# A macaron block with hybrid sparse attention on one Trainium2 core: attention's TensorE order held as written, position adds on GpSimd, compression jobs and first loads rearranged

## The chip, the cores and the metric

The kernel runs on one core of one Trainium2 chip. The metric is device time in microseconds of a run. Three runs of the kernel before took 1013.84 (median), 1013.3 and 1014.18. One execution was profiled; it is the source of all rows below.

## The reference

One transformer layer on 512 tokens of width 1024, float32. Everything is computed at float32 accuracy.

```python
x = x + 0.5 * swiglu(rmsnorm(x, norm_ffn1), w_gate1, w_up1, w_down1)      # 1024 -> 2816 -> 1024
x = x + hybrid_mixer(rmsnorm(x, norm_mix), w_in, ..., w_out, rel_bias)
x = x + 0.5 * swiglu(rmsnorm(x, norm_ffn2), w_gate2, w_up2, w_down2)
return rmsnorm(x, norm_final)

# hybrid_mixer: h @ w_in gives q, k, v of 8 MoBA heads (width 64), q of 8 NSA heads,
# two groups each of raw, selected and window k and v, and 24 gates
def compress(raw, pos, w1, w2):                # blocks of 32 tokens, every 16: 31 blocks
    blocks = raw[:, :, idx] + pos
    return silu(blocks.reshape(B, G, n_cmp, 32 * dh) @ w1) @ w2
# NSA: gates[0] * softmax over the 31 compressed blocks
#    + gates[1] * softmax over selected blocks of ks, vs + gates[2] * softmax over a window of kw, vw
# MoBA: softmax over the selected blocks and the own block; both with a relative position bias
# o = concat(heads) @ w_out
```

With 512 tokens every block is selected, so both the selected and the window branch are causal attention over all tokens.

## The kernel before, in words

**Products.** A float32 product is made of three matmuls (`mm3`, L86 to L89: L87, L88 and L89 are its three) on a high and a low part of each factor. A weight chunk is loaded by SyncE into one of three `raw` buffers; `halves` splits it: `whi` by ScalarE (ACT, L81), `wlo` by VectorE (DVE, L82), or by GpSimd (POOL) once `side[0]` is set, which is so during attention. Activations `x` are kept as eight tiles of 128 features by 512 tokens, and as pairs `xo` (high, low).

**The FFNs.** `Ffn.go` (L380 to L413) writes a list of steps out in order, with loads, sums and splits started ahead by fixed costs, and holds TensorE to that order: `tc.manual_schedule(engines={PE})`. `begun` (L416) makes the first steps, the six plain blocks, and hangs "posts" on them: work for other engines that is issued behind a given step. `sums_of_x` (L187) and `blocks_of_x` make what the later, mixed blocks need; `squares_of_tokens`, `roots` and `rows_of_roots` make 1/rms: a reciprocal on DVE (L150) and eight transpositions of it on TensorE into `pR` (L156). FFN1's first loads are written out by hand on SyncE's queue: `first_x` and `first_w`, then the four token tiles, then the third weight and x4 to x7.

**The mixer's projections.** All products of the normalized x with `w_in`, the compression and the output product are "jobs": a load and a generator that yields after each `mm3`. `stream` runs the jobs of the lists `pre`, `fill` and `last`, loading two ahead. `proj(i, then)` gives one 128-feature projection `pp`; `token_major` gives values `vn` and `vm` (tiles `pv`, copied with a factor by ACT L683 and DVE L684). `compress` gives for k and v each a projection whose `blocks` add the positions (L711, eight adds on DVE into a `raw` buffer), four hidden jobs (`pc`, ending in a silu into `hid`, L735 to L737), and `second`: two transpositions into `pct` (L745), splits, and a small product `pck`. `moved` (L607) copies halves of partitions by SyncE's queue: eight moves for a k (`stack_k`), four for a q pair (`stack_q`). The list `pre` is run to its end, `need("vc")`, before attention begins; in it the hidden jobs alternate with projections.

**Attention.** 72 steps of `chunks_of_head`: three for each of 24 passes (NSA heads 8 to 15 with ks and kw, MoBA heads 0 to 7), and four more of `cmp_pair` for the compressed branch. Each has a logits part (TensorE L900, L901 into `ps_s`; DVE L908 adds the bias `tb` and reduces to a maximum; ACT L910 exponential; DVE L915 reciprocal; POOL L921 gating), a turn (transpositions into `ps_t`, L930, copied to `th` by ACT L933 and `tl` by DVE L934), and values (L93, L94 into `po`). The loop issues the logits of step i, the turn of step i-4 and the values of step i-7, and after each a number of `mm3` of the job list, by the table `share`. So the job list fills TensorE between attention's parts. `ahead` and `need` force jobs that a head wants. In the kernel before, the program's scheduler, not this loop alone, sets the order of all engines here.

Of the kernel before, what the change touches and what calls it, by code (L numbers as in the profile page):

```python
# [18 lines left out]
NK = D // 128  # L19
# [13 lines left out]
def block_kernel(ctx: ExitStack, tc: tile.TileContext, A: dict, out: bass.AP):  # L33
# [382 lines left out]
    def begun(ffn, w, posts):  # L416

        steps = [s for f in range(0, PLAIN, 3) for s in ffn.plain(range(f, f + 3))]
        sums = [(at, lambda k=k: ffn.sums_of_x(k)) for k, at in enumerate((4, 6, 8, 10))]
        blocks = [(at, lambda k=k: ffn.blocks_of_x(k)) for k, at in enumerate((4, 18, 18, 23))]  # L420
        for at, post in posts + sums + blocks:
            steps[at].post.append(post)
        fills = ffn.down(w, range(PLAIN), half_added, "mm", 2)
        return steps + fills[:LEAD], fills[LEAD:]
# [46 lines left out]
    with ExitStack() as ph:  # L471
# [31 lines left out]
        first_w(1, [slice(0, 8)], nc.sync)  # L503
        tokens = [ffn.raw().rearrange("p a b c -> p (a b c)") for _ in range(NT)]
        for i in range(NT):
            nc.sync.dma_start(tokens[i], A["x"][i * 128:(i + 1) * 128])
        first_w(2, [slice(0, 8)], nc.sync)
        for k in range(4, NK):
            first_x(k)
# [23 lines left out]
        def then(d, p):  # L533
# [4 lines left out]
        steps, fills = begun(ffn, A["wd1"], [  # L538
            (1, squares_of_tokens), (2, lambda: roots(0, ss[:, 0])), (3, lambda: rows_of_roots(0, "mm")),
# [18 lines left out]
    with ExitStack() as ph:  # L558
# [140 lines left out]
        def compress(which):  # L699
# [3 lines left out]
            def blocks(p):  # L703
                tv = scaled(p, None).rearrange("p (n s) -> p s n", s=16)
                xt = chunk((16, 64))
                xv = xt.rearrange("p l (g n) -> p l g n", g=2)
                nc.gpsimd.memset(xv[:, :, :, 31:32], 0.0)
                for g in range(2):
                    for l in range(2):
                        for e in range(2):  # L710
                            nc.vector.tensor_tensor(  # L711
                                xv[half(l), 8 * e:8 * e + 8, g, 0:31], tv[half(g), l:16:2, e:e + 31],
                                pos[half(g), which, 16 * e + l:16 * e + 16:2].unsqueeze(2).to_broadcast([64, 8, 31]),
                                ALU.add)
                for l0 in range(0, 16, 4):
                    t = akt().rearrange("p (l e n) -> p l e n", l=4, e=2)
                    nc.scalar.activation(t[:, :, 0], xt[:, l0:l0 + 4], AF.Copy)
                    nc.vector.tensor_tensor(t[:, :, 1], xt[:, l0:l0 + 4], f32(t[:, :, 0]), ALU.subtract)
                    xc.extend(t[:, l].rearrange("p e n -> p (e n)") for l in range(4))
# [235 lines left out]
        def cmp_pair(pair):  # L955
# [38 lines left out]
            def values():  # L994
# [14 lines left out]
        pre = [kproj, *vn, khid[0], proj(10, nsa_k("ks")), khid[1], vm[0], khid[2], vproj, khid[3], vm[1], ksec,  # L1009
               vhid[0], vm[2], vhid[1], proj(11, nsa_k("kw")), vhid[2], proj(12, nsa_q(0)), vhid[3], vm[3], vsec]  # L1010
        fill = [proj(12 + i, nsa_q(i)) for i in range(1, 4)]
        for i in range(4):
            fill += [proj(2 * i, moba_t("q", i)), proj(2 * i + 1, moba_t("k", i))]
            if i == 2:
                fill += [w_out(d, 4, 8) for d in range(NK)]
# [29 lines left out]
        need("vc")  # L1045
# [29 lines left out]
        for i in range(len(steps) + 7):  # L1075
            for j, lag in enumerate((0, 4, 7)):
                if 0 <= i - lag < len(steps):
                    steps[i - lag][j]()
                run(max(0, int(target[i] + share[i] * (j + 1) / 3) - done[0]))
            if i in starts:  # L1080
                ahead(starts[i])
        for _ in work:
            pass
# [4 lines left out]
    with ExitStack() as ph:  # L1088
# [7 lines left out]
        steps, fills = begun(ffn, A["wd2a"], [  # L1096
            (2, lambda: roots(2, sums_of_squares("mm"))), (3, lambda: rows_of_roots(2, "mm"))])
# [156 lines left out]
```

## Time and profile before

| what | value |
|---|---|
| runs | 1013.3, 1013.84, 1014.18 us |
| profiled execution: time | 1012.73 us |
| profiled execution: span of its instructions | 1010.9 us |
| mean granted TensorE clock | 0.995 |
| TensorE matmuls | 5944 |
| first matmul of attention's stage, first of FFN2 | 434.04 us, 653.35 us |

All stamps are microseconds from the first instruction of the span. The order of stages is FFN1 to about 355, projections and compression to 434, attention to 653, FFN2 and the last norm to the end. A row of a timeline reads: start, duration, engine, line of the code, operation, what it writes and reads, shapes; in brackets the idle time just before it and what ended it. A window row reads: its bounds, its length, the busy time of PE (matmuls), PEld (weight loads), DVE, ACT and POOL with their counts, the granted TensorE clock, the DMA engines' busy share and GB/s.

### The profile page before, as it was taken

Reading aid. Unit: us, or ns where it says so; the run is one execution under the profiler, and the core shown is the slowest. Engines: PE = TensorE matmul, PEld = TensorE weight load, DVE = VectorE, ACT = ScalarE, POOL = GpSimd, SP = SyncE. Lnnn points to the kernel's source line nnn. Section 1 sums busy time; section 2 is a strip of 40 time slices with the busy share of each in tenths; the row PEclk is TensorE's granted clock in tenths of the full one; section 3 lists DMA queues with packets and bytes.
Section 4 is the critical chain, followed back from the end, with each engine's and each line's share of the span. In section 5 each row is a group of like instructions: output and inputs, shape, how many; then the busy total and the mean of one; then the engine's idle time right before and its main releaser. Section 6 shows DMA issues by size and latency. Waiting matters only on the chain.

```text
span 1010.9 us, 15557 instructions
## 1 busy us (share of the span) xinstructions
PE 983.3 (97%) x5944; PEld 862.5 (85%) x5944; DVE 718.7 (71%) x1135; ACT 504.8 (50%) x869; POOL 131.9 (13%) x167
## 2 busy tenths in 40 slices
PE   9999999999999999999999999889999999999997
PEld 7789989999999888788778787778899999999995
DVE  5986676777775675578787866777957777767743
ACT  7554343444433453467676856635534443444444
POOL 0000000000000220035554462600000000000002
PEclk9999999999999999999999999999999999999999
DMA  8533266333211135652132433353243323332102
GB/s 313 219 120 99 90 188 186 110 99 109 88 60 42 45 93 170 192 178 74 48 95 70 123 102 84 120 213 105 84 126 104 105 88 103 124 122 87 43 1 84
DMA packets 45742, 113.86 MB, mean 113 GB/s; under 512 B 10049, under 2 KB 14866, under 8 KB 45668
## 3 DMA queue, kind: packets, MB, share of 16 engines
q1 hardware_dynamic: 45380, 112.73, 36.0%
q8 instruction: 47, 0.77, 0.3%
q14 instruction: 27, 0.22, 0.1%
q10 hardware_dynamic: 288, 0.14, 0.1%
HBM read 100.08 MB, written 5.30 MB: 104 GB/s over the span
## 4 chain that ended last, share of the span: by engine, by line
PE 82%; DVE 6%; DMA 4%; ACT 2%; issue 2%; POOL 1%; SPq 1%; DVEq 0%; ACTq 0%; POOLq 0%
PE pd L87 8%; PE pd L88 8%; PE pd L89 8%; PE pu L89 6%; PE pu L87 6%; PE pu L88 6%; PE pw L87 4%; PE pw L88 4%; PE pw L89 4%; PE pgu L89 3%; PE pgu L87 3%; PE pgu L88 3%; PE pp L87 2%; PE pp L88 2%; PE pp L89 2%
## 5 line engine op out<-in xcount | busy, mean ns | idle before, releaser
L197 ACT ACTIVATE sph<-aw 128x1024 fp32r<-128x1024 f32 x114 | 120.9, 1061 | 237.0 <-PE pu L88 118.6
L81 ACT ACTIVATE whi<-raw 128x1024 fp32r<-128x1024 f32 (+3 forms) x115 | 111.9, 975 | 124.5 <-PE pd L88 30.7
L198 DVE TENSOR_TENSOR spl<-aw,sph 128x1024 fp32r<-128x1024 f32 x114 | 139.3, 1222 | 36.6 <-ACT sph L197 36.5
L82 DVE TENSOR_TENSOR wlo<-raw,whi 128x1024 fp32r<-128x1024 f32 (+3 forms) x91 | 110.9, 1222 | 28.8 <-ACT whi L81 28.0
L88 PE MATMUL pd<-h,whi 128*128 128x512 f32 x320 | 126.4, 395 | 0.0
L87 PE MATMUL pd<-h,whi 128*128 128x512 f32 x320 | 126.2, 394 | 0.0
L89 PE MATMUL pd<-h,wlo 128*128 128x512 f32 x320 | 125.2, 391 | 0.0
L89 PE MATMUL pu<-th,spl 128*128 128x256 f32 x384 | 106.9, 278 | 0.0
L87 PE MATMUL pu<-th,sph 128*128 128x256 f32 x384 | 106.9, 278 | 0.0
L88 PE MATMUL pu<-tl,sph 128*128 128x256 f32 x384 | 106.8, 278 | 0.0
L287 DVE TENSOR_TENSOR aw<-aw 128x1024 f32<-128x1024 f32 x64 | 78.1, 1220 | 33.1 <-DMA aw<-in_wgu 33.1
L469 DVE SCALAR_TENSOR_TENSOR x<-pd,x 128x512 f32<-128x512 f32 x72 | 49.4, 689 | 45.8 <-PE pd L89 45.6
L89 PE MATMUL pgu<-xo,wlo 128*128 128x512 f32 x192 | 74.9, 390 | 1.6 <-DVE wlo L82 1.6
L88 PEld LDWEIGHTS pu<-tl,sph 128*128 128x128 f32 x384 | 72.6, 189 | 4.0
L87 PEld LDWEIGHTS pu<-th,sph 128*128 128x128 f32 x384 | 72.1, 188 | 4.3
L87 PE MATMUL pgu<-xo,whi 128*128 128x512 f32 x192 | 75.3, 392 | 0.4 <-ACT xo L123 0.4
L88 PE MATMUL pgu<-xo,whi 128*128 128x512 f32 x192 | 75.0, 390 | 0.6 <-DVE xo L124 0.6
L89 PEld LDWEIGHTS pu<-th,spl 128*128 128x128 f32 x384 | 72.1, 188 | 0.0
L89 PEld LDWEIGHTS pd<-h,wlo 128*128 128x128 f32 x320 | 60.2, 188 | 13.4
L89 PE MATMUL pw<-xo,spl 128*128 128x256 f32 x256 | 70.9, 277 | 0.0
L87 PE MATMUL pw<-xo,sph 128*128 128x256 f32 x256 | 70.8, 277 | 0.0
L88 PE MATMUL pw<-xo,sph 128*128 128x256 f32 x256 | 70.8, 277 | 0.0
(254 smaller groups left out, 2432.7 us busy)
## 6 DMA issues: line engine op xcount, KB each, us to landing
aw<-in_wgu SPq DMA_DIRECT2D x64, 512.0 KB, 3.9
raw<-in_wgu SPq DMA_DIRECT2D x23, 512.0 KB, 4.6
raw<-in_wd SPq DMA_DIRECT2D x22, 512.0 KB, 3.7
raw<-in_wd2a SPq DMA_DIRECT2D x18, 512.0 KB, 3.7
raw<-in_w_a SPq DMA_DIRECT2D x16, 512.0 KB, 3.6
raw<-in_w SPq DMA_DIRECT2D x8, 512.0 KB, 3.7
aq<-xo SPq DMA_DIRECT2D x32, 128.0 KB, 2.3
raw<-in_w_o SPq DMA_DIRECT2D x16, 256.0 KB, 2.6
```

Of the source, the lines that this page charges most:

```text
L81: nc.scalar.activation(hi[:, s], src[:, s], AF.Copy)
L82: (nc.gpsimd if side[0] else nc.vector).tensor_tensor(lo[:, s], src[:, s], f32(hi[:, s]), ALU.subtract)
L87: nc.tensor.matmul(p, w[0], v[0], start=first, stop=False, skip_group_check=again)
L88: nc.tensor.matmul(p, w[0], v[1], start=False, stop=False, skip_group_check=again)
L89: nc.tensor.matmul(p, w[1], v[0], start=False, stop=last, skip_group_check=again)
L197: nc.scalar.activation(hi, v, AF.Copy)
L198: nc.vector.tensor_tensor(lo, v, f32(hi), ALU.subtract)
L287: nc.vector.tensor_tensor(to, x, y, op)
L469: nc.vector.scalar_tensor_tensor(xs[d], p, 0.5, xs[d], ALU.mult, ALU.add)
```

## The change

- **TensorE's order in attention.** The loop stands in `tc.manual_schedule(engines={PE})`; other engines are still scheduled. The table `share` gives MoBA steps 0.6 for 0.85, drops 2.0 after each MoBA start, adds 3.0 after heads 1, 3 and 5 begin, and 1.2 to the last steps.
- **Jobs.** The hidden jobs of k start later, so that two other jobs stand ahead; the last two of v stand side by side at the end; `vsec`, the second part of v's compression, goes from the end of `pre` into `fill`. A job `marked` ends `pre`. Half of the output jobs of pair 2 go behind pair 3. The splits and moves of the NSA q pairs 2 and 3 are put off to heads 11 and 13.
- **Position adds.** The eight adds of a `blocks` go from DVE to GpSimd, and from a `raw` buffer to the `spare` tiles that `halves_of_rows` uses.
- **FFN starts.** 1/rms is posted two steps later in FFN1 and its rows one step later in FFN2; sums of x begin at step 6 and 5 for 4. FFN1's third weight, x4 to x7 and the second half of block 0 are loaded ahead of the tokens.

```diff
-    def begun(ffn, w, posts):
+    def begun(ffn, w, first, posts):
-        sums = [(at, lambda k=k: ffn.sums_of_x(k)) for k, at in enumerate((4, 6, 8, 10))]
-        blocks = [(at, lambda k=k: ffn.blocks_of_x(k)) for k, at in enumerate((4, 18, 18, 23))]
+        sums = [(first + 2 * k, lambda k=k: ffn.sums_of_x(k)) for k in range(4)]
+        blocks = [(at, lambda k=k: ffn.blocks_of_x(k)) for k, at in enumerate((first, 18, 18, 23))]
...
         first_w(1, [slice(0, 8)], nc.sync)
+        first_w(2, [slice(0, 8)], nc.sync)
+        for k in range(4, NK):
+            first_x(k)
+        ffn.early[0, 1] = chunk((8, 128))
+        nc.sync.dma_start(ffn.early[0, 1], A["wgu1"][0][:, 1].rearrange("p a b c -> p (a b) c"))
         tokens = [ffn.raw().rearrange("p a b c -> p (a b c)") for _ in range(NT)]
...
-        first_w(2, [slice(0, 8)], nc.sync)
-        for k in range(4, NK):
-            first_x(k)
...
-            (1, squares_of_tokens), (2, lambda: roots(0, ss[:, 0])), (3, lambda: rows_of_roots(0, "mm")),
+            (3, squares_of_tokens), (4, lambda: roots(0, ss[:, 0])), (5, lambda: rows_of_roots(0, "mm")),
...
             def then(p):
                 t = scaled(p, 0.125)
-                got["n", pair] = stack_q(t)
+                got["t", pair] = t
+                if pair < 2:
+                    nsa_split(pair)
             return then
+        def nsa_split(pair):
+            got["n", pair] = stack_q(got["t", pair])
...
-                xt = chunk((16, 64))
-                xv = xt.rearrange("p l (g n) -> p l g n", g=2)
-                            nc.vector.tensor_tensor(
-                                xv[half(l), 8 * e:8 * e + 8, g, 0:31], tv[half(g), l:16:2, e:e + 31],
+                xt = [f32(v).rearrange("p (l n) -> p l n", l=8) for v in spare[which]]
+                            nc.gpsimd.tensor_tensor(
+                                xv[half(l), :, g, 0:31], tv[half(g), l:16:2, e:e + 31],
...
-        pre = [kproj, *vn, khid[0], proj(10, nsa_k("ks")), khid[1], vm[0], khid[2], vproj, khid[3], vm[1], ksec,
-               vhid[0], vm[2], vhid[1], proj(11, nsa_k("kw")), vhid[2], proj(12, nsa_q(0)), vhid[3], vm[3], vsec]
-        fill = [proj(12 + i, nsa_q(i)) for i in range(1, 4)]
+        pre = [kproj, *vn, proj(10, nsa_k("ks")), vm[0], khid[0], vproj, khid[1], vm[1], khid[2],
+               proj(11, nsa_k("kw")), khid[3], vm[2], ksec, vhid[0], proj(12, nsa_q(0)), vhid[1], vm[3], vhid[2], vhid[3],
+               (None, marked)]
+        fill = [proj(13, nsa_q(1)), vsec, proj(14, nsa_q(2)), proj(15, nsa_q(3))]
...
-            if i == 2:
-                fill += [w_out(d, 4, 8) for d in range(NK)]
+            if i >= 2:
+                fill += [w_out(d, 4, 8) for d in range(4 * i - 8, 4 * i - 4)]
...
+            if h in (11, 13):
+                need(("t", (h - 7) // 2))
+                nsa_split((h - 7) // 2)
...
-        need("vc")
+        need("pre")
...
-        share = [0.65 if i < n_nsa else 0.85 for i in range(len(steps) + 7)]
+        share = [0.65 if i < n_nsa else 0.6 for i in range(len(steps) + 7)]
-                if i >= n_nsa:
-                    share[i + 1] += 2.0
+            if starts.get(i) in (1, 3, 5):
+                share[i + 1] += 3.0
+        for i in range(len(steps) - 3, len(steps) + 7):
+            share[i] += 1.2
...
+        with tc.manual_schedule(engines={mybir.EngineType.PE}):
+            for i in range(len(steps) + 7):
...
-            (2, lambda: roots(2, sums_of_squares("mm"))), (3, lambda: rows_of_roots(2, "mm"))])
+            (2, lambda: roots(2, sums_of_squares("mm"))), (4, lambda: rows_of_roots(2, "mm"))])
```

Where the instructions stand now, at three places.

TensorE, the first steps of attention. `ps_s` are logits, `pp` a projection's matmuls that fill, `ps_t` the first turn. The turn's last transposition reads `lp_4256`, the softmax of the third logits. Before, 29 other rows follow those logits, and then come:

```order
L87 MATMUL pp_4435<-xo_3456,whi_4181 128x512
L900 MATMUL ps_s_4299<-kvn_4056,aq_4117 128x512
L901 MATMUL ps_s_4299<-kvn_4058,aq_4117 128x512
L88 MATMUL pp_4435<-xo_3457,whi_4181 128x512
L89 MATMUL pp_4435<-xo_3456,wlo_4182 128x512
L87 MATMUL pp_4435<-xo_3467,whi_4181 128x512
L88 MATMUL pp_4435<-xo_3468,whi_4181 128x512
L89 MATMUL pp_4435<-xo_3467,wlo_4182 128x512
L87 MATMUL pp_4604<-xo_3352,whi_4220 128x512
L88 MATMUL pp_4604<-xo_3353,whi_4220 128x512
L930 MATMUL ps_t_4287<-ident_84,lp_4256 128x128
```

In the changed kernel, from the third logits (`ps_s_4215`, whose softmax is `lp_4216`) on:

```order
L908 MATMUL ps_s_4215<-kvn_3746,aq_4089 128x512
L909 MATMUL ps_s_4215<-kvn_3748,aq_4089 128x512
L908 MATMUL ps_s_4223<-kvn_3955,aq_4089 128x128
L909 MATMUL ps_s_4223<-kvn_3957,aq_4089 128x128
L908 MATMUL ps_s_4223<-kvn_3955,aq_4089 128x256
L909 MATMUL ps_s_4223<-kvn_3957,aq_4089 128x256
L87 MATMUL pp_4211<-xo_3361,whi_4163 128x512
L88 MATMUL pp_4211<-xo_3362,whi_4163 128x512
L89 MATMUL pp_4211<-xo_3361,wlo_4164 128x512
L908 MATMUL ps_s_4237<-kvn_3955,aq_4089 128x384
L909 MATMUL ps_s_4237<-kvn_3957,aq_4089 128x384
L938 MATMUL ps_t_4247<-ident_84,lpn_4182 128x128 x2
```

The turn comes nine rows after the third logits, and its four transpositions stand together: two more rows of it, the second reading `lp_4216`, follow.

ACT at the same place. `vm` are the copies of the last value chunk, `whi` splits of weights, `hid` the hidden layer of v's compression, L918 (L910 before) the exponentials. Before:

```order
L735 ACTIVATE hid_4133<-pc_3970 64x256
L737 ACTIVATE hid_4133<-hid_4133 64x256
L81 ACTIVATE whi_4181<-raw_4179 128x1024
L683 ACTIVATE vm_4167<-pv_3795,rc1_94 128x8x64
L683 ACTIVATE vm_4168<-pv_3796,rc1_94 128x8x64
L683 ACTIVATE vm_4169<-pv_3797,rc1_94 128x8x64
L683 ACTIVATE vm_4170<-pv_3798,rc1_94 128x8x64
L81 ACTIVATE whi_4220<-raw_4218 128x1024
L750 ACTIVATE hh_4188<-pct_4185 128x128
L756 ACTIVATE w2h_4194<-w2_4192 128x128
L910 ACT_TABLE_LOAD
L910 ACTIVATE lpn_4229,m_4234<-lpn_4229,m_4234 128x128
```

In the changed kernel, from the last copy on:

```order
L690 ACTIVATE vm_4144<-pv_3769,rc1_94 128x8x64
L81 ACTIVATE whi_4163<-raw_4161 128x1024
L81 ACTIVATE whi_4207<-raw_4205 128x1024
L743 ACTIVATE hid_4175<-pc_4047 64x256
L81 ACTIVATE whi_4398<-raw_4396 128x1024
L918 ACT_TABLE_LOAD
L918 ACTIVATE lpn_4182,m_4187<-lpn_4182,m_4187 128x128
L918 ACTIVATE lpn_4182,m_4187<-lpn_4182,m_4187 128x256
L918 ACTIVATE lpn_4196,m_4187<-lpn_4196,m_4187 128x384
L745 ACT_TABLE_LOAD
L745 ACTIVATE hid_4175<-hid_4175 64x256
L918 ACT_TABLE_LOAD
```

The silu of `hid` stood ahead of the copies and of all exponentials; it stands now between the third and the fourth exponential of the first pass, with a table load on either side.

DVE at the start of FFN1. L187 are the sums of x, L82 splits of weights, L124 the low parts of x. Before:

```order
L124 SCALAR_TENSOR_TENSOR xo_196<-x6_76,gcol_69,xo_195 128x512
L187 SCALAR_TENSOR_TENSOR xa_310<-x0_70,gcol_69,R_100 128x512
L187 SCALAR_TENSOR_TENSOR xb_311<-x4_74,gcol_69,R_100 128x512
L187 SCALAR_TENSOR_TENSOR xa_363<-x1_71,gcol_69,R_100 128x512
L187 SCALAR_TENSOR_TENSOR xb_364<-x5_75,gcol_69,R_100 128x512
L187 SCALAR_TENSOR_TENSOR xa_405<-x2_72,gcol_69,R_100 128x512
L187 SCALAR_TENSOR_TENSOR xb_406<-x6_76,gcol_69,R_100 128x512
L124 SCALAR_TENSOR_TENSOR xo_200<-x7_77,gcol_69,xo_199 128x512
L448 TENSOR_TENSOR tabl_92<-tabs_89,tabh_91 33x16
L188 TENSOR_TENSOR xa_310<-xa_310 128x256
L82 TENSOR_TENSOR wlo_275<-raw_205,whi_274 128x1024
```

In the changed kernel:

```order
L124 SCALAR_TENSOR_TENSOR xo_198<-x6_76,gcol_69,xo_197 128x512
L124 SCALAR_TENSOR_TENSOR xo_202<-x7_77,gcol_69,xo_201 128x512
L82 TENSOR_TENSOR wlo_269<-raw_150,whi_268 128x1024
L446 TENSOR_TENSOR tabs_89<-tabs_89,far_90 32x16
L448 TENSOR_TENSOR tabl_92<-tabs_89,tabh_91 33x16
L150 RECIPROCAL rc0_93<-rc0_93 128x4
L82 TENSOR_TENSOR wlo_307<-raw_207,whi_306 128x1024
L82 TENSOR_TENSOR wlo_366<-raw_234,whi_365 128x1024
L187 SCALAR_TENSOR_TENSOR xa_341<-x0_70,gcol_69,R_100 128x512
L187 SCALAR_TENSOR_TENSOR xb_342<-x4_74,gcol_69,R_100 128x512
```

The six sums stood ahead of a split; three splits stand ahead of the sums now.

More of the change, by code (lines that the diff above doesn't have):

```diff
@@ L536, in then @@
             squares(tmp, d, "tmp", 3)
-        steps, fills = begun(ffn, A["wd1"], [
-            (1, squares_of_tokens), (2, lambda: roots(0, ss[:, 0])), (3, lambda: rows_of_roots(0, "mm")),
+        steps, fills = begun(ffn, A["wd1"], 6, [
+            (3, squares_of_tokens), (4, lambda: roots(0, ss[:, 0])), (5, lambda: rows_of_roots(0, "mm")),
             (12, make_rows)])
@@ L704, in blocks @@
                 tv = scaled(p, None).rearrange("p (n s) -> p s n", s=16)
-                xt = chunk((16, 64))
-                xv = xt.rearrange("p l (g n) -> p l g n", g=2)
[L707 to L711, printed above, removed]
-                                xv[half(l), 8 * e:8 * e + 8, g, 0:31], tv[half(g), l:16:2, e:e + 31],
+                xt = [f32(v).rearrange("p (l n) -> p l n", l=8) for v in spare[which]]
+                for e in range(2):
+                    xv = xt[e].rearrange("p l (g n) -> p l g n", g=2)
+                    nc.gpsimd.memset(xv[:, :, :, 31:32], 0.0)
+                    for g in range(2):
+                        for l in range(2):
+                            nc.gpsimd.tensor_tensor(
+                                xv[half(l), :, g, 0:31], tv[half(g), l:16:2, e:e + 31],
                                 pos[half(g), which, 16 * e + l:16 * e + 16:2].unsqueeze(2).to_broadcast([64, 8, 31]),
@@ L715, in blocks @@
                 for l0 in range(0, 16, 4):
+                    v = xt[l0 // 8][:, l0 % 8:l0 % 8 + 4]
                     t = akt().rearrange("p (l e n) -> p l e n", l=4, e=2)
-                    nc.scalar.activation(t[:, :, 0], xt[:, l0:l0 + 4], AF.Copy)
-                    nc.vector.tensor_tensor(t[:, :, 1], xt[:, l0:l0 + 4], f32(t[:, :, 0]), ALU.subtract)
+                    nc.scalar.activation(t[:, :, 0], v, AF.Copy)
+                    nc.vector.tensor_tensor(t[:, :, 1], v, f32(t[:, :, 0]), ALU.subtract)
                     xc.extend(t[:, l].rearrange("p e n -> p (e n)") for l in range(4))
@@ L1008, in block_kernel, with marked @@
         vm = token_major("vm", A["w_v"], 512, vm_tiles)
-        pre = [kproj, *vn, khid[0], proj(10, nsa_k("ks")), khid[1], vm[0], khid[2], vproj, khid[3], vm[1], ksec,
-               vhid[0], vm[2], vhid[1], proj(11, nsa_k("kw")), vhid[2], proj(12, nsa_q(0)), vhid[3], vm[3], vsec]
-        fill = [proj(12 + i, nsa_q(i)) for i in range(1, 4)]
+        def marked(w):
+            got["pre"] = True
+            yield
+        pre = [kproj, *vn, proj(10, nsa_k("ks")), vm[0], khid[0], vproj, khid[1], vm[1], khid[2],
+               proj(11, nsa_k("kw")), khid[3], vm[2], ksec, vhid[0], proj(12, nsa_q(0)), vhid[1], vm[3], vhid[2], vhid[3],
+               (None, marked)]
+        fill = [proj(13, nsa_q(1)), vsec, proj(14, nsa_q(2)), proj(15, nsa_q(3))]
         for i in range(4):
             fill += [proj(2 * i, moba_t("q", i)), proj(2 * i + 1, moba_t("k", i))]
-            if i == 2:
-                fill += [w_out(d, 4, 8) for d in range(NK)]
+            if i >= 2:
+                fill += [w_out(d, 4, 8) for d in range(4 * i - 8, 4 * i - 4)]
         both = []
@@ L1070, in block_kernel @@
                 share[i + 7] += 2.0
-                if i >= n_nsa:
-                    share[i + 1] += 2.0
+            if starts.get(i) in (1, 3, 5):
+                share[i + 1] += 3.0
+        for i in range(len(steps) - 3, len(steps) + 7):
+            share[i] += 1.2
         target = [sum(share[:i]) for i in range(len(share) + 1)]
[L1075 to L1083, printed above, removed]
+        with tc.manual_schedule(engines={mybir.EngineType.PE}):
+            for i in range(len(steps) + 7):
+                for j, lag in enumerate((0, 4, 7)):
+                    if 0 <= i - lag < len(steps):
+                        steps[i - lag][j]()
+                    run(max(0, int(target[i] + share[i] * (j + 1) / 3) - done[0]))
+                if i in starts:
+                    ahead(starts[i])
+            for _ in work:
+                pass
         xg = [got["x", d] for d in range(NK)]
@@ L1094, in block_kernel @@
         hs = ffn.hs
-        steps, fills = begun(ffn, A["wd2a"], [
-            (2, lambda: roots(2, sums_of_squares("mm"))), (3, lambda: rows_of_roots(2, "mm"))])
+        steps, fills = begun(ffn, A["wd2a"], 5, [
+            (2, lambda: roots(2, sums_of_squares("mm"))), (4, lambda: rows_of_roots(2, "mm"))])
         for f in range(PLAIN, NF, FP):
```

## The prediction

> **What bounds the kernel now.** I read the page's shares first, then windows by stage, then TensorE's waits, then timelines at the gaps.
>
> ```profile
> span 1010.9 us, 15557 instructions
> PE 983.3 (97%) x5944; PEld 862.5 (85%) x5944; DVE 718.7 (71%) x1135; ACT 504.8 (50%) x869; POOL 131.9 (13%) x167
> ```
>
> TensorE (PE) is busy 97% of the span, and the change leaves its 5944 matmuls alone. What can go is its idle time, 27.6 us, and time at a lowered clock. The windows by stage (columns: length, then busy time of PE, weight loads, DVE, ACT, POOL, then granted clock) say where that lies:
>
> ```profile
> 50.00:350.00 300.00, 300.00 (x1978) 272.67 (x1977) 211.48 (x246) 128.75 (x174) 4.90 (x6) 1.00 0.34 105
> 355.00:434.00 79.00, 74.55 (x396) 63.55 (x395) 49.02 (x67) 37.13 (x58) 6.44 (x5) 0.96 0.54 163
> 434.00:653.40 219.40, 209.97 (x1152) 172.83 (x1152) 168.62 (x441) 147.52 (x361) 110.38 (x139) 1.00 0.35 93
> 675.00:975.00 300.00, 300.00 (x1975) 273.23 (x1974) 217.75 (x266) 130.64 (x176) 0.00 (x0) 1.00 0.30 94
> 373.00:383.00 10.00, 7.64 (x29) 5.89 (x28) 7.46 (x15) 5.52 (x14) 0.00 (x0) 0.83 0.41 125
> 403.00:413.00 10.00, 7.91 (x28) 5.70 (x27) 6.12 (x11) 5.54 (x10) 0.00 (x0) 0.83 0.60 178
> ```
>
> The two FFNs lose nothing in their 300 us stretches. The projections before attention (355 to 434) lose 4.45 us at two places, both followed by a granted clock of 0.83. Attention (434 to 653.4) shows 9.4 us idle. The list of PE's waits (line, releaser, total, times, longest) gives the names:
>
> ```profile
> PE pR L156 <- DVE rc L150: 2.9, 1, 2.9
> PE ps_s L900 <- DVE m L908: 2.9, 9, 0.6
> PE pp L89 <- DVE wlo L82: 2.4, 1, 2.4
> PE pct L745 <- ACT hid L737: 1.8, 1, 1.8
> PE pgu L89 <- DVE wlo L82: 1.6, 1, 1.6
> ```
>
> Four single waits carry 8.7 us; attention's are many and short. The list understates a wait, because a matmul's shown duration overlaps the next one:
>
> ```profile
> 434.04 0.39 PE L87 MATMUL pp<-xo,whi 128*128 128x512 f32 x1
> 470.00 0.40 PE L88 MATMUL pp<-xo,whi 128*128 128x512 f32 x1
> 470.23 0.39 PE L89 MATMUL pp<-xo,wlo 128*128 128x512 f32 x1
> 653.35 0.39 PE L87 MATMUL pgu<-xo,whi 128*128 128x512 f32 x1
> ```
>
> Undisturbed 512-column matmuls start 0.23 us apart (470.00 and 470.23) and show 0.40. I therefore count losses from start to start. From the first of attention's 1152 matmuls (434.04) to the first after them (653.35), the excess of each spacing over that of its shape, taken where it passes 0.08 us, adds to 23 us: 9.4 visible, the rest inside shown durations. About 8 of it lies in 610 to 640, the rest mostly in 500 to 570.
>
> **FFN1's start.** Matmul 25.50 is followed by one at 27.44: 1.94 us where 0.23 is due, 1.7 lost.
>
> ```profile
> 25.50 0.39 PE L88 MATMUL pgu<-xo,whi 128*128 128x512 f32 x1
> 27.44 0.50 PE L89 MATMUL pgu<-xo,wlo 128*128 128x512 f32 x1 [1.56 <-DVE wlo L82]
> 26.18 1.21 DVE L82 TENSOR_TENSOR wlo<-raw,whi 128x1024 fp32r<-128x1024 f32 x1
> ```
>
> The DVE split at 26.18 stands behind six sums (L187, about 0.7 us each). In the changed order three weight splits stand ahead of those sums. The x and third-weight loads also move ahead of the tokens; the squares that need tokens are posted two steps later. I take the whole 1.7. Bounds: 0, if the token loads, now later, hold the rows of 1/rms; 3, if the earlier half of block 0 also removes small waits.
>
> **Projections: two stalls go, a small one comes.**
>
> ```profile
> 370.88 4.34 DVE L711 TENSOR_TENSOR raw<-t,pos 64x248 f32<-64x248 f32 x8
> L139 POOL TENSOR_TENSOR acc<-acc,sq 128x512 f32<-128x512 f32 x14 | 22.4, 1598 | 16.1 <-ACT sq L138 15.9
> 641.58 1.56 DVE L124 SCALAR_TENSOR_TENSOR xo<-x,gcol,xo 128x512 fp32r<-128x512 f32 x1 [0.80 <-ACT xo L123]
> 637.73 0.76 DVE L124 SCALAR_TENSOR_TENSOR xo<-x,gcol,xo 128x512 fp32r<-128x512 f32 x1 [0.33 <-ACT xo L123]
> ```
>
> The eight position adds hold DVE for 4.34 us, and the split that PE wants stands behind them. Idle 2.36 plus 0.17 x 10 of lost clock makes 4.1 us in the window 373 to 383. On GpSimd an add of 248 columns is not in the trace; by L139 (1.6 us for 512) it costs about 0.8, so eight cost 6.4, against a first consumer (the first hidden job) that now stands one projection plus one chunk of the value projection later, about 10 us of PE work. Without that cover the adds would cost 6.4 at each of two calls. The second stall (403 to 413: idle 2.09 plus 1.7 of clock, 3.8) is the silu of the hidden layer, read at once, together with weight loads queued behind eight moves. In the new job order the moves stand behind three loads, and the first silu has a value chunk and its own projection between. I take both away, 7.9, and add 0.45 at the last value chunk, where two hidden jobs now stand side by side: 7.4 saved (bounds 3 and 8).
>
> A DVE op took 0.76 alone and 1.56 beside a GpSimd op (641.58). By the Trainium skill, "SBUF — State Buffer", section "SBUF: two separate sides", a DVE op with two SBUF inputs and a GpSimd op that reads SBUF lock each other out wholly; the two durations agree. By rows, DVE would stand still for up to 2 x 6.4 = 12.8 us; it is busy 49 of 79 us here, so I put that at nothing as long as the 10 us cover holds.
>
> **FFN2's start.**
>
> ```profile
> 664.96 0.39 PE L89 MATMUL pgu<-xo,wlo 128*128 128x512 f32 x1
> 668.29 0.38 PE L156 MATMUL pR<-ident,rc 128*128 128x128 f32 x1 [2.95 <-DVE rc L150]
> 666.92 1.23 DVE L287 TENSOR_TENSOR aw<-aw 128x1024 f32<-128x1024 f32 x1 [5.79 <-DMA aw<-in_wgu]
> ```
>
> 3.33 us pass where 0.23 is due. The reciprocal waits behind a DVE sum (666.92), which waits for a load. In the new order DVE keeps that sequence, but PE takes the transposition one step, 12 matmuls or 2.7 us, later: 2.7 saved, 0.4 left (bounds 0, were the load later too, and 3.1).
>
> **Attention.** Its PE order is now that of the code. Where the scheduler spread transpositions among a projection's matmuls (a third logits matmul and the transposition that reads it 40 rows apart), the new order has nine rows between them. Three places of the first steps:
>
> ```profile
> 433.22 2.42 ACT L683 ACTIVATE vm<-pv,rc 128x512 fp32r<-128x512 f32 x4
> 435.52 1.07 ACT L81 ACTIVATE whi<-raw 128x1024 fp32r<-128x1024 f32 x1
> 439.31 0.31 ACT L756 ACTIVATE w2h<-w 128x128 fp32r<-128x128 f32 x1 [2.56 <-DMA w<-in_w]
> 439.64 1.28 ACT L910 ACT_TABLE_LOAD   x1
> 440.93 0.40 ACT L910 ACTIVATE lpn<-lpn,m 128x128 f32<-128x128 f32 x1
> 443.75 0.68 DVE L908 CUSTOM_DVE_ANT_0 lp<-ps_s,tb 128x512 f32<-128x512 f32 x1
> 444.47 0.72 ACT L910 ACTIVATE lp<-lp,m 128x512 f32<-128x512 f32 x1 [0.17 <-DVE m L908]
> 447.77 0.77 POOL L921 TENSOR_SCALAR lp<-lp,m,gates 128x512 f32<-128x512 f32 x1 [0.73 <-DVE m L915]
> 430.94 0.42 ACT L737 ACTIVATE hid<-hid 64x256 f32<-64x256 f32 x1 [1.29 <-DVE hid L736]
> ```
>
> *The start.* T is the end of the last value chunk on PE. ACT begins the four copies 0.8 us before T (433.22 against PE's 434.04) and ends them at T+1.6. Behind them the changed ACT order has three splits of 1.07 and one copy of the hidden layer (about 0.4): T+5.2. Then a table load of 1.28, the first exponentials (1.5), a load, the silu (0.42), a load, and the wide exponential (0.72 and its sum's read-out, 0.2): T+11.9. Reciprocal and gating (0.77) end at T+12.8. PE's own work up to the first transposition (two hidden jobs, ten logits matmuls, six of a projection) is 5.1 us. So PE waits about 7.5 us in two pieces, where it now waits for none; after pieces of 2.36 and 1.76 above the clock fell, costing 1.7, and I add 1.2 here. 8.7 in all; bounds 4 (the silu taken later) and 12.
>
> ACT's own row before the load ends at 439.62 and the exponential starts at 440.93, 1.29 after the load starts: nothing but the load is paid. By the Trainium skill, "ScalarE: Activation LUTs", section "What ACT_TABLE_LOAD costs", a switch costs some 1.28 us of load plus 1.38 of drain; the second half does not show here.
>
> *The value side of compression* now runs inside attention, with its two products directly behind its transposition:
>
> ```profile
> 435.94 0.33 PE L745 MATMUL pct<-ident,hid 64*128 64x64 f32 x2
> 441.23 0.19 PE L87 MATMUL pck<-w2h,hh 128*32 128x64 f32 x1
> ```
>
> Before, 5.3 us of other work lay between (435.94 to 441.23). Now the copies stand on that path: 3.2 (bounds 2 and 5).
>
> *Each step's chain.* Wide logits to transposition takes reduce 0.68, exponential 0.72 and 0.2, reciprocal 0.2, gating 0.77, some 2.6 plus handovers, 3 to 5 us with work in between. PE work between is 3.2 to 6.4 us in the new order while projections fill in: 4 us over the 48 NSA steps (bounds 0 and 8).
>
> *Moved halves.* A MoBA pair's k and q pass through SyncE:
>
> ```profile
> 384.95 5.71 SPq L607 DMA_DIRECT2D kvn<-xo  x8
> aq<-xo SPq DMA_DIRECT2D x32, 128.0 KB, 2.3
> ```
>
> Eight moves take 5.71 us to issue, 2.3 more to land; with splits of 2 us and the first two of q's, head 6's first logits come 11.4 us after its k projection. The order puts 3.0 us of PE work between, and the waits of the steps there take another 4: about 4 lost. Heads 2 and 4, with more between, lose 1 and 2.5: 7.5 in all (bounds 2 and 28, below).
>
> *The tail.* Heads 5 to 7 have hardly any fill left; 1.7 to 2.4 us of work stand against the chain's 3: 4 us, and 1.5 of lowered clock.
>
> After: 8.7 + 3.2 + 4 + 7.5 + 5.5 = 28.9, against 23 of the same count before: +5.9.
>
> **The sum.** -1.7 - 7.4 - 2.7 + 5.9 = -5.9. The profiled execution took 1012.73 (span 1010.9 and 1.8 around it), so 1006.8; the median of the runs, 1013.84, lies 1.1 above, so 1007.9. Attention's losses S decide: the net is S - 34.8.
>
> **Rivals.**
> - *The waits hide* (13%). ACT, DVE and POOL are busy 67%, 77% and 50% of attention, so outside the start there is room. Only the start and the value side remain, S = 11.9: 991. Against it: the nine logits waits in today's list, at looser order.
> - *A wash* (12%): S between 32.8 and 36.9, the gains of the other stages used up by attention: 1014.
> - *Slower: the moved halves decide* (18%). PE cannot pass a waiting logits matmul, and fill stands behind it. If each of the seven pairs after the first waits like head 6, S = 28.9 - 7.5 + 28 = 49.4: 1028. It decides from S = 36.9, which three more such starts than I count nearly reach. For it: one SyncE queue for loads and moves; against it: the NSA pairs' splits are brought forward.
> - *GpSimd's adds and DVE lock each other and the cover is gone* (2%): 12.8 more, 1021.
> - *A table switch costs its load's 1.28 twice* (3%), three times at the start: 3.8 more, 1011.7, about the edge of no change. The drain that the Trainium skill, "ScalarE: Activation LUTs", section "What ACT_TABLE_LOAD costs", adds would do that; the row at 440.93 speaks against it.
> - That the order isn't held is excluded by PE's new order.
>
> **Chances and range.** The forecast, S from 22 to 32.8, has 52%. One kernel's measurement tells about 0.2%, 2 us. Faster by more: 52 + 13 = 65%. Within: 12 + 3 = 15%. Slower: 18 + 2 = 20%. From 993 to 1019 lie the forecast, the wash, the table and lock cases' nearer parts, half of the hiding case and a third of the slower one; about 20% is left out. The forecast's own range is 1001 to 1012.
>
> **What would show it.** PE's waits at 25.5 and at the FFN2 rows, and both clock dips in 373 to 413, should be gone. In the first 15 us of attention one or two waits of 3 to 5 us for the gated softmax (L929) should stand, with table loads on ACT around a silu. Attention should last 222 to 229 us. Waits of logits on moved halves at every pair, with a granted clock under 1.00 in attention, would make the prediction wrong on the slow side; attention under 215 us on the fast side.

## The result, and the profile after

The changed kernel takes 1019.65 us (median of 4 runs, 1019.0 to 1021.67) against 1013.57 (1013.26 to 1014.18): a ratio of 1.0063, 95% interval 1.0045 to 1.0080. It is slower by 6.1 us; 5.9 us faster was forecast. The profiled execution took 1019.0 with a span of 1017.2.

```profile
span 1017.2 us, 15533 instructions
PE 982.8 (97%) x5944; PEld 866.3 (85%) x5944; DVE 716.8 (70%) x1117; ACT 511.9 (50%) x871; POOL 153.2 (15%) x187
PEclk9999999999999999979999999999999999999999
```

TensorE's busy time and its matmul count are as before (983.3, 5944). The third row is the granted clock in 40 slices: one slice, that of 432 to 458, stands at 7 tenths, where before none was below 9.

The stages are cut at three starts on PE. Before, the first projection matmul comes at 353.76 and FFN2's first matmul at 653.35 (shown above):

```profile
353.76 0.39 PE L87 MATMUL pp<-xo,whi 128*128 128x512 f32 x1
```

In the changed kernel, the same two places:

```profile
351.67 0.39 PE L87 MATMUL pp<-xo,whi 128*128 128x512 f32 x1
662.93 0.39 PE L87 MATMUL pgu<-xo,whi 128*128 128x512 f32 x1
```

FFN1 ends 2.1 us earlier. From there to FFN2 it takes 311.3 us for 299.6: 11.7 more. FFN2 and the last norm take 354.3 for 357.6: 3.3 less. The sum is +6.3, the difference of the spans. Inside the middle part the list of PE's waits has changed at its top (line, releaser, total, times, longest):

```profile
PE ps_t L938 <- DVE tl L942: 5.1, 6, 1.5
PE ps_t L938 <- POOL lp L929: 4.3, 5, 2.4
PE ps_s L909 <- DMA ak<-xo: 3.5, 2, 2.3
PE ps_t L938 <- POOL lpn L929: 2.7, 3, 2.2
PE pck L87 <- ACT w2h L764: 2.7, 2, 1.8
PE pck L88 <- DVE w2l L765: 2.0, 1, 2.0
```

The four single waits shown of before (rc, two wlo, hid, 8.7 us) are gone. In their place stand waits of transpositions (`ps_t`) for softmax and for the copies of an earlier turn (`tl`), of logits for moved halves (`ak`), and of the compression's small product (`pck`; the two long ones, 1.8 and 2.0, are the value side's). Windows of the changed kernel (length, busy time of PE, weight loads, DVE, ACT, POOL, granted clock):

```profile
351.70:424.70 73.00, 72.13 (x402) 62.54 (x401) 45.66 (x55) 38.57 (x61) 23.37 (x26) 1.00 0.57 174
424.70:662.90 238.20, 213.42 (x1152) 177.99 (x1151) 170.65 (x436) 153.20 (x363) 115.42 (x141) 0.96 0.31 85
425.00:460.00 35.00, 25.98 (x129) 20.91 (x128) 19.78 (x64) 21.74 (x52) 15.55 (x19) 0.80 0.27 85
435.00:442.00 7.00, 6.98 (x28) 5.65 (x29) 3.73 (x13) 3.86 (x12) 2.70 (x5) 0.64 0.11 28
452.40:457.50 5.10, 5.10 (x24) 4.52 (x22) 1.74 (x7) 1.76 (x6) 0.00 (x0) 0.54 0.58 175
500.00:560.00 60.00, 55.10 (x322) 46.56 (x323) 49.86 (x135) 39.91 (x101) 28.19 (x38) 1.00 0.27 71
```

The projections lose 0.9 us of idle time where they lost 4.45, and no clock. The first 35 us of attention hold most of the damage: 9 us idle, and a clock of 0.80. The fourth and fifth rows show how: PE is busy throughout, but at 0.64 and 0.54 of its clock, directly behind two stalls. Time is lost twice, in the wait and in the slow stretch behind it.

The start of attention on PE, from the last logits ahead of the first turn:

```profile
428.39 0.34 PE L909 MATMUL ps_s<-kvn,aq 128*128 128x384 f32 x1
430.93 0.33 PE L938 MATMUL ps_t<-ident,lpn 128*128 128x128 f32 x1 [2.20 <-POOL lpn L929]
431.46 0.33 PE L938 MATMUL ps_t<-ident,lpn 128*128 128x128 f32 x1 [0.21 <-POOL lpn L929]
432.10 0.33 PE L938 MATMUL ps_t<-ident,lpn 128*128 128x128 f32 x1 [0.31 <-POOL lpn L929]
434.86 0.47 PE L938 MATMUL ps_t<-ident,lp 128*128 128x128 f32 x1 [2.43 <-POOL lp L929]
434.99 0.77 PE L87 MATMUL pp<-xo,whi 128*128 128x512 f32 x1
435.56 0.63 PE L88 MATMUL pp<-xo,whi 128*128 128x512 f32 x1
435.99 0.63 PE L89 MATMUL pp<-xo,wlo 128*128 128x512 f32 x1
```

PE stands before the transpositions with `pp` matmuls ready behind them. When it gets to these, they come 0.43 us apart (435.56 to 435.99) where 0.23 is due. From start to start, less 0.175 us for the logits and 0.107 for a transposition, the four waits cost 6.0 us. ACT in the same time:

```profile
427.01 1.28 ACT L918 ACT_TABLE_LOAD   x1
429.91 1.28 ACT L745 ACT_TABLE_LOAD   x1
431.20 0.42 ACT L745 ACTIVATE hid<-hid 64x256 f32<-64x256 f32 x1
431.64 1.28 ACT L918 ACT_TABLE_LOAD   x1
432.93 0.72 ACT L918 ACTIVATE lp<-lp,m 128x512 f32<-128x512 f32 x1
```

The chain is the one that the prediction worked out: splits, a table load, exponentials, a load, the silu, a load, the wide exponential.

### The profile page after: what moved, and what is told of

Its sections match the earlier page's. It is cut to its first block, busy times and chain, and to the rows that moved or that the text cites. A ratio compares the mean times of both kernels' runs of the same rounds, so it can differ in the third digit from the quotient of the medians.

```text
span 1017.2 us, 15533 instructions
## 1 busy us (share of the span) xinstructions
PE 982.8 (97%) x5944; PEld 866.3 (85%) x5944; DVE 716.8 (70%) x1117; ACT 511.9 (50%) x871; POOL 153.2 (15%) x187
## 5 line engine op out<-in xcount | busy, mean ns | idle before, releaser
L198 DVE TENSOR_TENSOR spl<-aw,sph 128x1024 fp32r<-128x1024 f32 x114 | 139.3, 1222 | 37.0 <-ACT sph L197 36.9
L82 DVE TENSOR_TENSOR wlo<-raw,whi 128x1024 fp32r<-128x1024 f32 (+3 forms) x89 | 110.2, 1240 | 20.4 <-ACT whi L81 18.9
```

Source lines behind the costliest of these rows:

```text
L82: (nc.gpsimd if side[0] else nc.vector).tensor_tensor(lo[:, s], src[:, s], f32(hi[:, s]), ALU.subtract)
L198: nc.vector.tensor_tensor(lo, v, f32(hi), ALU.subtract)
```

## The experiments

Theory 1: the loss is the bare start of attention (silu, table loads and the value side without cover). Theory 2: the held order as such costs, all along, since PE can't pass a waiting instruction. Each experiment was compared with the kernel before on the same chip; its medians there were 1012.2 to 1013.1 (1013.57 beside the changed kernel), so a difference between two rows of the table is good to a microsecond or two. "Loss" below is the excess of PE's start-to-start spacing over that of the shape (0.23 us for 512 columns, 0.107 for a transposition), summed where it passes 0.15 us, from the first logits to FFN2 (for the kernel before from 434.04). Its size hangs on the spacings taken: with 0.23, 0.175 and 0.115 us for 512, 384 and 256 columns and 0.107 for narrower matmuls, single cells come out up to 2.2 us lower (attention 15.4 before, 34.5 changed, 16.2 in e3), and the differences between kernels up to 1.8.

| kernel | us, median | ratio to before, 95% interval | loss to 460 | 460 to 600 | behind 600 |
|---|---|---|---|---|---|
| before | 1013.6 | 1 | 1.1 | 9.7 | 7.3 |
| changed | 1019.65 | 1.0063 (1.0045 to 1.0080) | 15.6 | 13.5 | 9.7 |
| e1 rest only | 1004.26 | 0.9923 (0.9901 to 0.9945) | 1.3 | 8.3 | 8.8 |
| e2 before, held | 1030.07 | 1.0179 (1.0147 to 1.0212) | 5.6 | 18.7 | 11.1 |
| e3 changed, free | 1001.16 | 0.9893 (0.9871 to 0.9915) | 6.0 | 8.4 | 5.2 |
| e4 cover | 1022.94 | 1.0111 (1.0087 to 1.0135) | 7.7 | 22.5 | 10.2 |
| e5 first held | 1009.75 | 0.9977 (0.9961 to 0.9992) | 15.2 | 6.1 | 5.6 |
| e6 later held | 1020.02 | 1.0076 (1.0049 to 1.0104) | 11.0 | 15.1 | 9.4 |
| e7 lag | 1019.22 | 1.0063 (1.0038 to 1.0087) | 14.4 | 15.6 | 8.2 |
| e8 FFNs only | 1007.82 | 0.9955 (0.9938 to 0.9972) | | | |
| e9 free, adds on DVE | 1002.07 | 0.9880 (0.9855 to 0.9905) | | | |
| e10 free, old jobs | 1002.92 | 0.9885 (0.9863 to 0.9908) | | | |
| e11 held, splits on DVE | 1017.15 | 1.0041 (1.0024 to 1.0058) | 14.0 | 10.6 | 10.6 |
| e12 held, more fill | 1023.5 | 1.0092 (1.0066 to 1.0118) | 10.2 | 19.3 | 11.3 |
| e13 free, splits on DVE | 1003.12 | 0.9897 (0.9849 to 0.9945) | | | |
| e14 free, old shares | 1002.74 | 0.9896 (0.9855 to 0.9938) | | | |

**e1, the change without attention.** The loop, `share`, `nsa_q`, the output jobs and `vsec` as before; the FFN starts, the adds and the rest of `pre` as changed.

> The kernel before, with the changed FFN starts, the GpSimd adds and the new job order ahead of attention, but attention as it was: its order left to the scheduler, the old share table, the value side's second part (vsec) ahead of attention, the q splits of pairs 2 and 3 not put off. Both theories: the gains of the three other stages measured between the two traces, 2.1 + 7.3 + 3.3 = 12.7, stay: about 1001 us (999 to 1004). If it comes out near 1008 or more, the gains outside attention are partly given back inside it even in the old order.

Measured 1004.26, just outside the 999 to 1004: 8.2 under the kernel before on that chip, two thirds of the 12.7. The two FFNs keep their gain (1.8 and 3.3 us in the trace). The projections keep 3.8 us of loss (1.8 in the changed kernel, 9.0 before, in the same count); attention's is as before, 18.4 for 18.1. Most of what else is missing of the 12.7 lies in spacings below the count. So most of the other stages' gain is there without the new attention.

**e2, the held order alone, put on the kernel before.**

```diff
-        for i in range(len(steps) + 7):
-            for j, lag in enumerate((0, 4, 7)):
+        with tc.manual_schedule(engines={mybir.EngineType.PE}):
+            for i in range(len(steps) + 7):
+                for j, lag in enumerate((0, 4, 7)):
...
```

> The kernel before, with nothing changed but that attention's TensorE order is held as its loop writes it. Theory 1 (the loss is the bare start of attention: silu, table loads and vsec without cover): the old job list has vsec and more ahead of attention, so holding costs little: 1014 to 1022 us. Theory 2 (a held order makes every step wait, and the loss of about 20 us is spread): about 1030 us or more, with waits of transpositions throughout.

Measured 1030.07, 17 to 18 us slower. Theory 2. The old list has one table load at the start and no silu between the exponentials, and its loss there is 5.6 us; most of the loss sits behind 460 (29.8 for 17.0), and some 3 us more are lost ahead of its first logits (438.23).

**e3, the changed kernel without the held order.**

```diff
-        with tc.manual_schedule(engines={mybir.EngineType.PE}):
+        with ExitStack():
```

> The changed kernel without the held order: the scheduler orders TensorE in attention again, all else as changed. Theory 1: the start's waits shrink only as far as the scheduler puts projection matmuls in them: 1003 to 1010 us. Theory 2: nearly the whole 20 us come back: 999 to 1003 us.

Measured 1001.16: 18.5 us come back (17.2 by the two ratios), and the version is 1.1% faster than the kernel before (interval 0.9% to 1.3%). e9, e10, e13 and e14, free as well, lie within 2 us of it. The waits on lp and lpn are gone from its list. Its waits:

```profile
PE pck L87 <- ACT w2h L764: 2.7, 2, 1.9
PE ps_s L908 <- DVE m L916: 1.3, 7, 0.2
PE pw L88 <- DVE kvn L867: 1.3, 1, 1.3
PE po L93 <- ACT th L941: 1.2, 5, 0.4
```

Between the third logits and the transposition that reads their softmax stand now 23 `pp` matmuls, which the scheduler took from jobs that the loop issues later:

```profile
431.78 0.39 PE L908 MATMUL ps_s<-kvn,aq 128*128 128x512 f32 x1
...
432.92 0.40 PE L89 MATMUL pp<-xo,wlo 128*128 128x512 f32 x1
433.16 0.39 PE L87 MATMUL pp<-xo,whi 128*128 128x512 f32 x1
...
439.32 0.38 PE L938 MATMUL ps_t<-ident,lp 128*128 128x128 f32 x2
```

7.5 us lie between logits and transposition, all of it work, and no bracket stands in the row. In the held order the same span was 8.4 us, 6.0 of them lost to waits.

**e4, cover ahead of attention, order held.**

```diff
-               (None, marked)]
+               proj(13, nsa_q(1)), vsec, (None, marked)]
-        fill = [proj(13, nsa_q(1)), vsec, proj(14, nsa_q(2)), proj(15, nsa_q(3))]
+        fill = [proj(14, nsa_q(2)), proj(15, nsa_q(3))]
```

> The changed kernel, order still held, but one projection (13) and vsec are taken from the fill to the end of the list ahead of attention, so that 24 matmuls stand between the last hidden job and the first turn. Theory 1: the start's two stalls of 6.1 us, vsec's 4.2 us and the low clock behind both (some 7 us) go: 1003 to 1008 us. Theory 2: only part of the start goes and the waits after 460 us stay: 1012 to 1016 us.

Measured 1022.94, outside of both. The start's loss fell by 8 us as theory 1 had it, and the total still rose: behind 460 it is 9.5 us more. The projection put at the start is missing later, and the clock behind 460 is lower: 0.94 from 460 to 600, where the changed kernel had 1.00.

**e5 and e6, held in one part only.** The loop's body is a function; `range(13)` or the rest stands in the held block.

```diff
...
+        with tc.manual_schedule(engines={mybir.EngineType.PE}):
+            turns_of(range(13))
+        turns_of(range(13, len(steps) + 7))
```

> The changed kernel with attention's order held for the first 13 loop turns only (to about 460 us), free behind. Theory 1, in its new form (of the 18.5 us that holding costs, the start, where idle time and low clock are 11.6 us more than in the free run, has most): about 1013 us (1011 to 1015). Theory 2 (the loss is spread over all steps, the start has its share by length): about 1004 us.

> The mirror: the first 13 turns free, the rest held. Theory 1: 1007 to 1009 us (the remaining 7 of 18.5). Theory 2: 1016 us or more, most of the loss.

Measured 1009.75 and 1020.02. Holding the first 13 turns costs 8.6 us over e3, between the two theories; holding all costs 9.9 more; and holding only the later turns costs as much as holding all, which is theory 2 and more than the loss by place explains: the parts don't add. The window of the first 35 us, of e6 and then of e3, shows what the free start lacks in e6:

```profile
425.00:460.00 35.00, 27.96 (x161) 22.90 (x161) 23.58 (x73) 25.50 (x61) 17.48 (x21) 0.91 0.34 100
```

```profile
425.00:460.00 35.00, 31.62 (x179) 26.46 (x177) 20.75 (x68) 24.27 (x56) 22.18 (x23) 0.97 0.40 120
```

The first turns are free in both, but where the later ones are held PE issues 161 matmuls in these 35 us for 179, idles 7.0 us for 3.4, and gets less clock. What fills a gap in a free order is work from later turns. That the held block keeps this work back was not tested by itself; it would explain e6.

**e7, one more step between a logits part and its turn.**

```diff
...
-                for j, lag in enumerate((0, 4, 7)):
+                for j, lag in enumerate((0, 5, 8)):
```

Two lines go with it: one more buffer for the narrow softmax (`lpn`, five for four), and the table shifted by the added step.

> The changed kernel, held, with turns issued 5 and values 8 steps behind their logits, for 4 and 7 (one more narrow softmax buffer for it). If the held order loses because PE stands before a turn whose softmax isn't done, one more step of PE work (about 2 us) ahead of each turn takes away most of the waits on lp and lpn (8.5 us) and some low clock: 1008 to 1013 us. If the waits are on DVE's and ACT's queues as such (they come late by whatever they are behind), it moves little: 1017 to 1022 us.

Measured 1019.22: no gain. The loss behind waits on lp and lpn falls from 8.5 to 5.7 us, that behind waits on `tl` grows from 6.0 to 9.2: where softmax is less late, the next turn stands before a buffer that DVE hasn't read yet.

**e8, the FFN starts alone.** All hunks of the diff in `begun`, in FFN1's loads and in the two calls, on the kernel before.

> The kernel before with the FFN starts alone changed (1/rms posted later, sums later, loads reordered, the second half of block 0 early). From the traces: 2.1 less ahead of the projections and 3.3 less behind attention, so about 5.4 under the kernel before. Against the second: the kernel before with the held order had FFN2 as short (347.1 for 350.5) without that edit, only because attention ended later; if that is the cause, 2 to 3 us under.

Measured 1007.82, 4.4 us under the kernel before on that chip, nearer the first figure: both starts gain by themselves (1.7 and 3.3 us in the trace). In its trace the transposition of 1/rms in FFN2 has no bracket.

**e9 and e10, the two edits of the projections apart (order free).** e9 puts the adds back on DVE (`nc.vector` for `nc.gpsimd` in `blocks`); e10 restores the old job order (less `vsec`).

> The version without the held order (1001.2 us), with the position adds back on DVE, still into the spare tiles. If the first stall ahead of attention went because the first hidden job now stands some 10 us later, the engine of the adds is worth nothing: 1000 to 1002.5 us. If it went because DVE is free of 2 x 4.3 us of adds, a split is late again: 1004 us or more.

> The version without the held order, adds on GpSimd, but the old order of the jobs ahead of attention (less vsec, which stays in the fill). If the job order removed the stalls, both come back in part, the first shorter since the adds no longer hold DVE: 1004 to 1008 us. If the move of the adds did it, only the silu's stall of 3.8 us at most returns: 1001 to 1004 us.

Measured 1002.07 and 1002.92: 0.9 and 1.8 us over e3, less than a measurement here can tell. In this count the projections lose 2.5 and 3.1 us for e3's 1.8. In both, nearly all of the stalls are gone; together the two edits bring little more. But both runs keep the adds in the `spare` tiles, where the kernel before took a `raw` buffer from the weight loads, and both keep `vsec` out of `pre`. No run puts these back, so that they did part of it isn't excluded.

**e11 and e13, attention's weight splits on DVE** (`side[0] = False`), held and free.

> The changed kernel, held, with the weight splits of attention on DVE instead of GpSimd (45 us of GpSimd work become some 22 us of DVE work). If the held order's waits on the low halves of turns (6 us, and what follows) come from DVE operations that GpSimd's splits stretch (one of 0.67 us took 1.78 beside one), it gets faster: 1011 to 1016 us. If they come from queue order alone, DVE's extra work makes it slower or the same: 1019 to 1024 us.

> The version without the held order (1001.2 us), with attention's weight splits on DVE instead of GpSimd. In the held order the same edit brought 2.5 us. If the gain was DVE operations that no longer run beside GpSimd's splits, it is there in the free order too, smaller since PE passes waits: 999 to 1001 us. If it was only another queue order, nothing or a loss by DVE's extra work: 1001 to 1004 us.

Measured 1017.15, between the two theories, and 1003.12. That is 2.5 us less in the held order (the intervals of the two ratios overlap) and 2 more, within noise, in the free one. The figure is a net one. The stretched operations are short again in e11 (L986, shown at the end, takes 0.17 us), but DVE's added splits stand in its queue: the waits for `pck` come to 5.0 us for 4.7. So the edit removes a small part of the held order's loss; what the stretching alone costs stays open.

**e12, more fill for the first turns, order held.**

```diff
-        fill = [proj(13, nsa_q(1)), vsec, proj(14, nsa_q(2)), proj(15, nsa_q(3))]
+        fill = [proj(13, nsa_q(1)), proj(14, nsa_q(2)), vsec, proj(15, nsa_q(3))]
+        for i in range(1, 5):
+            share[i] += 3.0
```

> The changed kernel, held, with twelve more fill steps (3 in each of turns 1 to 4) and vsec one projection later, so that some 8 us of projection stand ahead of the first turn. If the start's loss is its own, it falls by the 8.6 us that holding the start cost: 1010 to 1013 us. If fill is a stock and what is used early is missing later, most comes back as waits behind 460 us: 1016 to 1020 us.

Measured 1023.5, slower than both. The start lost 5.4 us less and the rest 7.4 more. One place in its trace shows how early fill comes back:

```profile
571.03 0.27 PE L94 MATMUL po<-tl,kvn 128*128 128x128 f32 x1
572.39 0.51 PE L87 MATMUL pw<-o,whi 128*128 128x512 f32 x1 [1.08 <-ACT o L863]
574.74 0.50 PE L88 MATMUL pw<-o,whi 128*128 128x512 f32 x1 [1.85 <-DVE o L867]
```

With twelve more steps used at the start, the job list reaches the output product at the moment when the head that it reads has just ended: 3.7 us from 571.03 to 574.74, which the changed kernel doesn't have.

**e14, the old share table, order free.**

> The version without the held order, with the old share table (0.85 in MoBA, 2.0 after each MoBA start, none of the new additions). If the scheduler sets the order by its own rule and the loop only offers work, the table is worth nothing: 1000 to 1002.5 us. If the table carries part of the 3.1 us by which this version is below the one with the old attention (1004.3), it comes out at 1003 us or more.

Measured 1002.74, between the two figures, 1.6 over e3 and within noise. Where the scheduler orders PE, no effect of the table's numbers is shown.

## Why the prediction was wrong, point by point

**FFN1's start** was right: 1.7 forecast, 2.1 measured. **FFN2's start** was right: 2.7 forecast with 0.4 left, 3.3 measured; the transposition came without a wait. **The projections** were right in size: 7.4 forecast, and their loss went from 9.0 to 1.8 in the count of the table. What removed it is less clear-cut than the text had it: in e9 and e10 either edit does without the other.

**The step that failed is attention's sum**, "28.9, against 23 of the same count before: +5.9". In a consistent count it is 38.8 against 18.1: +20.7. By e3, holding the order is nearly the whole of it: without it attention's loss is 19.6. By place, 11.9 was booked up to 460 and 15.6 measured, 7.5 from there to 600 and 13.5 measured, 9.5 behind 600 and 9.7 measured. Three things were wrong in that step.

- *The 23 of before.* It held spacings of 0.08 to 0.15 us over their shape, of which the 28.9, a sum of waits, held none. Such small ones, as behind each change from transpositions to large matmuls, are in both orders (counted from 0.08 on, 25.5 to 28.6 before, not 23, and 43.7 to 47.0 now, by the spacings taken). Like with like, 18.1 was to be subtracted in place of 23: a difference of 4.9 us.
- *The low clock.* 1.2 was booked at the start and 1.5 in the tail. The windows 435 to 442 (0.64) and 452.4 to 457.5 (0.54) cost 7.0 x 0.36 and 5.1 x 0.46, 4.9 us together, and a third stretch follows the moved halves at 614 (0.57 for 4 us, 1.7). The waits themselves were forecast well: 7.5 at the first turn, 6.0 measured; 3.2 for the value side, 4.2.

```profile
614.00:618.00 4.00, 4.00 (x20) 3.53 (x18) 2.31 (x8) 3.19 (x9) 0.00 (x0) 0.57 0.36 101
```

- *The steps in the middle.* "PE work between is 3.2 to 6.4 us ... 4 us over the 48 NSA steps" compared PE's work with one softmax chain. It left out that PE also waits for DVE's copy of the turn before (`tl`). That copy is last in 6.3 us of the waits between 460 and 600 (11.7 in the lower count), where the softmax itself is last in some 1.8. It comes behind other work on ACT and on DVE:

```profile
499.42 0.33 PE L909 MATMUL ps_s<-kvn,aq 128*128 128x384 f32 x1
501.12 0.52 PE L938 MATMUL ps_t<-ident,lpn 128*128 128x128 f32 x3 [1.37 <-DVE tl L942]
```

ACT and DVE in the same time:

```profile
499.30 0.46 ACT L941 ACTIVATE th<-ps_t 128x384 fp32r<-128x384 f32 x1
499.90 0.56 DVE L916 CUSTOM_DVE_ANT_0 lpn<-ps_s,tb 128x384 f32<-128x384 f32 x1 [1.11 <-PE ps_s L909]
500.42 0.56 DVE L942 TENSOR_TENSOR tl<-ps_t,th 128x384 fp32r<-128x384 f32 x1
```

DVE's reduce waits 1.1 us for the logits that PE starts at 499.42; the copy stands behind it, and PE's next transposition waits for the copy. The high part `th`, which the copy reads, is done at 499.76, so about 0.6 of the 1.37 us is the place behind the reduce; the rest is the copy itself, the handovers and ACT, which took `th` up behind its exponentials. 460 to 600 lost 13.5 us for the 4, the 1 and the 2.5 that were booked there.

**The moved halves** were near: heads 4 and 6 lost 5.4 us between them (6.5 booked). The larger part, head 6's:

```profile
610.60 0.30 PE L908 MATMUL ps_s<-ak,aq 128*128 128x128 f32 x1 [1.28 <-DMA ak<-xo]
613.23 0.30 PE L909 MATMUL ps_s<-ak,aq 128*128 128x128 f32 x1 [2.33 <-DMA ak<-xo]
```

The slower rival's mechanism, these waits at every pair, is not what happened: only these two heads waited. Its condition, S above 36.9, was met at 38.8 by the steps in the middle and the clock. The rival of the GpSimd adds fell: they took 15.9 us there, and the projections lost 1.8. (The row at 637.73 that the prediction calls alone has GpSimd splits beside it; ten wholly alone in that trace take 0.74 to 0.75, so the 0.76 stands for an undisturbed one all the same.) The rival on table switches fell too: exponential 432.93 starts 1.29 after its load, with no further gap, as in the trace of before and against the drain that the Trainium skill, "ScalarE: Activation LUTs", section "What ACT_TABLE_LOAD costs", adds.

What the prediction didn't weigh is what the scheduler's order saves as a whole: the losses of the old order were taken as that order's fault. e2 answers it with 17 to 18 us. Open stays how much of the 9.9 us by which e5 is below the changed kernel is each of: coupled queues, fill held back, and moved halves. e7 speaks against a short distance as the main part, e11 against GpSimd's splits.

## What to carry to other kernels

An in-order engine whose order is held by hand waits for everything that is late on four other queues, and the longest of these waits were followed by some microseconds at a lower clock. Holding was dear where every step depends on three other engines; the FFNs, held in both kernels, lose nothing in their 300 us stretches, though no run frees them. Fill work is a stock: moving it by hand to one gap (e4, e12) opened larger ones later (9.5 us for 7.9, 7.4 for 5.4). Before an order is replaced, ask what the old one hides: look for long runs of filler between a producer and its consumer, and price their absence with the clock behind the stall.

## What the runs showed of the hardware that was not expected

Time lost to the clock came to about half of the wait before it: behind 6.0 us of stalls in four pieces the clock was 0.64 for 7 us (2.5 lost), and behind 4.2 us of waits 0.54 for 5 (2.3 lost). Some DVE operations beside GpSimd's splits took far longer than alone, even one on 8 elements per partition. DVE in the changed kernel:

```profile
449.20 1.27 DVE L986 TENSOR_SCALAR mc<-mc 128x8 f32<-128x8 f32 x1
534.74 1.78 DVE L867 TENSOR_TENSOR o<-to,u 64x512 fp32r<-64x512 f32 x1 [0.44 <-ACT u L866]
624.90 0.67 DVE L867 TENSOR_TENSOR kvn<-to,u 64x512 fp32r<-64x512 f32 x1
```

GpSimd:

```profile
448.09 2.35 POOL L82 TENSOR_TENSOR wlo<-raw,whi 128x1024 fp32r<-128x1024 f32 x1 [1.95 <-ACT whi L81]
533.58 2.41 POOL L82 TENSOR_TENSOR wlo<-raw,whi 128x1024 fp32r<-128x1024 f32 x1 [2.23 <-ACT whi L81]
```

L986 ends at 450.47, 0.03 us behind the split. All four of its executions end 0.03 us behind a split, after 0.22 to 2.37 us; in e11, where DVE makes attention's splits, all four take 0.16 to 0.17. L867 ends 0.53 behind its split, and without a split beside it takes 0.67. That is how an operation looks that stands still until the other is done. Not every operation does: beside the first split shown, the copy `tl` at 448.73 takes its usual 0.56. The Trainium skill, "SBUF — State Buffer", section "SBUF: two separate sides", gives such a lock for DVE operations with two SBUF inputs, which L867 is, or in a two-port mode; L986 reads one tile. A position add took 0.99 us on GpSimd (16 in 15.9 us), for 0.54 on DVE (8 in 4.34).
